# RWKV chain of a two-block layer: only the state's products stay in it, those with V and of the outputs are batched outside

## Chip, cores and metric

The program runs on one NeuronCore of one Trainium2 chip. The metric is the device time of that core in microseconds (us), as the median of several executions. All data are float32.

## What is computed

The kernel runs two transformer blocks on 512 tokens of width 1024. The first one (neighbourhood attention, gated linear attention, convolutional feed-forward) is not touched. In the second one, a projection feeds windowed attention and a bidirectional RWKV-7 time mix with 8 heads of 64; its outputs go through gates, a merge and two more feed-forward stages. The part that the change concerns is this scan, for both directions:

```python
def step(state, inp):
    r_t, w_t, k_t, v_t, a_t, b_t = inp
    sa = jnp.einsum('dbhij,dbhj->dbhi', state, a_t)
    state = (state * w_t[..., None, :] + sa[..., :, None] * b_t[..., None, :]
             + v_t[..., :, None] * k_t[..., None, :])
    y = jnp.einsum('dbhij,dbhj->dbhi', state, r_t)
    return state, y
```

The kernel does it in chunks of 64 tokens. Within a chunk the tokens' mutual effect is a triangular system, and between chunks a 64x64 state per head and direction is handed on.

## The kernel before

`block2` handles the 8 heads as four pairs `p`; the two heads `e` of a pair lie on partitions 0 to 63 and 64 to 127 (slices `H[e]`, and `O[e]` for the other half). Each pair goes through three functions.

`prep(p)` (line 1006) computes decays, keys and gates for both directions `d`. For each half of the chunks it makes `Z` (decayed queries) and `BK` (decayed keys), and their products `pP` (line 1090) on TensorE. VectorE masks these into the matrices `M[e]` (line 1092). `BKT` is `BK` transposed. The diagonal 32x32 blocks of `M` go through a DRAM scratch `scL` (line 1097) into `LF` and `XH` (lines 1112 and 1114). Then 60 VectorE operations in a row solve the triangular systems (`sx` at line 1120, `XH` at 1122). Preparation's PSUM tiles come from the pool `ps_` (tag "s", two buffers).

`finish(p)` (line 1125) writes the inverses `XH` to DRAM (`scX`) and reads them back into `M` (line 1136). It joins the 32-blocks on TensorE: `pax` (line 1144), `pt1` (1151), `pg2_` (1156). `LF` is used again here as working space.

`chain(p)` (line 1159) transposes V into `VU` (the V half; the other half takes U) and makes `W0`, the products with V (`pv`, line 1177). Then come eight dependent steps, in which direction 0 takes chunk s and direction 1 chunk 7-s:

- line 1191: `Z` times the old state `So`, into `pw`; line 1193: VectorE adds `W0`, giving `w`;
- line 1196: `M` times `w`, into `pu`; line 1199: ScalarE and VectorE copy one head each into `VU`;
- lines 1203 and 1205: an identity matmul of the old state and the product of `BKT` with `VU` (V and U at once, 128 rows) accumulate in `px`;
- lines 1226 and 1227: ScalarE and VectorE scale one direction each by the decay `PCs`, giving the new state `Sn`;
- `ymm()`: lines 1212 and 1214 make the step's outputs `py`, which lines 1218 and 1220 add into `Y`.

After the steps the outputs are normalised, transposed, gated and stored.

The order of the work is set by a list scheduler that sorts each engine's instructions by priority (program order, lowered by `low`) and readiness. It hands out the buffers of a pool's tag in program order. Program order is `prep(0)`, fill, `finish(0)`, `chain(0)`, `prep(1)`, fill, and so on. "Fill" (`fill`, line 1396) are weight matmuls at low priority: groups of `w_in_2` (line 251, 24 matmuls of 512 columns each, in two chunks of weights), and for pair 3 the `qkv` product (line 1277, 256 columns) with its norms (`qknorm`, lines 1296 to 1311). Each chunk's low part is made on GpSimd (line 203) and is loaded by SyncE's queue. After `chain(3)` comes the windowed attention (line 1313) with the last gate groups as fill.

Of the kernel before, what the change touches and what calls it, by code (L numbers as in the profile page):

```python
# [8 lines left out]
F32 = mybir.dt.float32  # L9
# [8 lines left out]
S = 512  # L18
# [138 lines left out]
class Ker:  # L157
# [768 lines left out]
    def block2(self, out):  # L926
# [79 lines left out]
        def prep(p):  # L1006
# [36 lines left out]
            for d in range(2):  # L1043
# [37 lines left out]
                for hf in ((0, 1), (1, 0))[d]:  # L1081
# [77 lines left out]
        def chain(p, st, u, PCs, XH, LF, M):  # L1159
            Y = rl.tile([128, 8, 64], F32, tag="Y", name=f"Y{p}")  # L1160
            vt = V[p]
            VU = rl.tile([128, 8, 128], F32, tag="VU", name=f"VU{p}")
            for h in range(2):
# [3 lines left out]
                for e in range(2):  # L1167
                    ev(e, VU[H[e], 4 * h:4 * h + 4, H[e]], px[:, :, H[e]])
            pbn = pc_.tile([128, 512], F32, tag="y", name=f"pbn{p}")
            nc.tensor.matmul(pbn, bones, u, start=True, stop=True)  # L1170
            nc.vector.tensor_tensor(vt, pbn, vt, ALU.mult)
            W0 = rl.tile([128, 2, 8, 64], F32, tag="W0", name=f"W0{p}")
            for d in range(2):
                pv = pc_.tile([128, 8, 64], F32, tag="y", name=f"pv{p}{d}")
                for cc in range(8):
                    for e in range(2):
                        nc.tensor.matmul(pv[O[e], cc, :], M[e][H[e], d, cc, 0:64], VU[H[e], cc, H[e]], start=True, stop=True)
                ev(d, W0[:, d], pv)
            Sn = None
            for s in range(8):  # L1180
# [26 lines left out]
                def ymm():
                    py = pc_.tile([128, 2, 64], F32, tag="y", name=f"py{p}{s}")
                    for d in range(2):
                        for e in range(2):  # L1210
                            if s > 0:
                                nc.tensor.matmul(py[H[e], d, :], zs[d][H[e], 64:128], So[H[e], d, :], start=True, stop=False)
                        for e in range(2):
# [380 lines left out]
```

## Time and profile before

| what | value |
|---|---|
| median of 3 runs | 1883.17 us |
| the runs | 1884.64, 1883.17, 1872.40 us |
| span of the profiled execution | 1873.3 us |
| busy: TensorE, VectorE, ScalarE, GpSimd | 96%, 57%, 41%, 10% of the span |

The profile is of one execution, and its span is its own time; it lies near the lowest of the three runs. Times in it are counted from the span's start. PE is the matmul part of TensorE, DVE is VectorE, ACT ScalarE, POOL GpSimd, SP SyncE, whose queue issues the DMAs. A float32 matmul shows as two records. The ends of matmuls are modelled, so their starts are read, and a busy PE need not be at its peak. PEclk is the share of full clock that TensorE was granted.

### The profile page before, as it was taken

How to read it: one execution, taken by the hardware profiler on the slowest of the kernel's cores; microseconds unless marked ns; L12 is line 12 of the kernel's file. 1: busy time of each engine (PE TensorE's matmuls, PEld its weight loads, DVE VectorE, ACT ScalarE, POOL GpSimd, SP SyncE). 2: the span in 40 equal slices, each digit the busy share in tenths (PEclk: the TensorE clock that was granted, in tenths of full speed). 3: DMA queues.
4: the chain of work that ended last, by engine and by line, in shares of the span. 5: the costliest groups of instructions: out<-in, count | busy, mean ns of one | idle time of the engine just before them, and what ended most of it. 6: DMA issues, size and time to landing. Idle time of an engine off the chain costs nothing.

```text
span 1873.3 us, 31022 instructions
## 1 busy us (share of the span) xinstructions
PE 1799.5 (96%) x11936; PEld 1506.6 (80%) x11936; DVE 1075.4 (57%) x2274; ACT 770.5 (41%) x1563; POOL 192.2 (10%) x217
## 2 busy tenths in 40 slices
PE   8999999989999999888789989999999999999998
PEld 7788888889998999866566768886678888888887
DVE  5644544787752677866746592437656553255445
ACT  6452434665442445653133432235434442234333
POOL 1000110110000001452211121112000000000000
PEclk9989989999999999998699997589999999999999
DMA  6111121653333334531221113112055333333334
GB/s 189 40 46 46 53 78 57 179 154 111 94 90 96 91 93 136 172 103 46 62 74 48 53 52 81 29 42 86 28 159 161 107 96 96 96 95 92 96 96 130
DMA packets 130789, 171.08 MB, mean 91 GB/s; under 512 B 44455, under 2 KB 59055, under 8 KB 130640
## 3 DMA queue, kind: packets, MB, share of 16 engines
q1 hardware_dynamic: 130640, 169.09, 31.1%
q8 instruction: 94, 1.54, 0.3%
q14 instruction: 55, 0.45, 0.1%
HBM read 155.42 MB, written 13.63 MB: 90 GB/s over the span
## 4 chain that ended last, share of the span: by engine, by line
PE 86%; DVE 7%; DMA 3%; issue 2%; ACT 2%; POOL 0%; SPq 0%; DVEq 0%; ACTq 0%; POOLq 0%
PE ps_w_ff L251 19%; PE ps_w_ffn_in L251 13%; PE ps_w_in L284 7%; PE ps_w_in L251 6%; PE ps_w_ffn_out L251 5%; PE ps_qkv L1277 3%; PE ps_w_out L251 2%; PE ps_w_ple_gate L251 2%; PE pP L1090 2%; PE ps_w_up_rwkv L251 1%; PE py L1214 1%; PE ps_w_up_attn L251 1%; PE ps_first L364 1%; PE paS L1350 1%; PE pS L632 1%
## 5 line engine op out<-in xcount | busy, mean ns | idle before, releaser
L203 DVE TENSOR_TENSOR wl_w_ff<-raw_w_ff,wh_w_ff 128x512 fp32r<-128x512 f32 x128 | 88.2, 689 | 131.6 <-ACT wh_w_ff L202 131.5
L202 ACT ACTIVATE wh_w_ff<-raw_w_ff 128x512 fp32r<-128x512 f32 x128 | 80.9, 632 | 194.7 <-PE ps_w_ff L251 185.9
L202 ACT ACTIVATE wh_w_in<-raw_w_in 128x512 fp32r<-128x512 f32 (+1 forms) x118 | 72.9, 623 | 101.9 <-PE ps_w_in L284 53.0
L203 POOL TENSOR_TENSOR wl_w_in<-raw_w_in,wh_w_in 128x512 fp32r<-128x512 f32 x60 | 82.0, 1371 | 254.6 <-ACT wh_w_in L202 192.2
L202 ACT ACTIVATE wh_w_ffn_in<-raw_w_ffn_in 128x512 fp32r<-128x512 f32 x96 | 60.1, 630 | 100.8 <-PE ps_w_ffn_in L251 87.4
L251 PE MATMUL ps_w_ff<-Yl,wh_w_ff 128*128 128x512 f32 x256 | 101.0, 395 | 0.0
L251 PE MATMUL ps_w_ff<-Yh,wh_w_ff 128*128 128x512 f32 x256 | 101.0, 395 | 0.0
L251 PE MATMUL ps_w_ff<-Yh,wl_w_ff 128*128 128x512 f32 x256 | 101.0, 395 | 0.0
L251 PE MATMUL ps_w_ffn_out<-Y_hi,wl_w_ffn_out 128*128 128x256 f32 (+1 forms) x256 | 83.5, 326 | 2.2 <-DVE wl_w_ffn_out L203 2.1
L251 PE MATMUL ps_w_ffn_out<-Y_hi,wh_w_ffn_out 128*128 128x256 f32 (+1 forms) x256 | 83.7, 327 | 0.0
L251 PE MATMUL ps_w_ffn_out<-Y_lo,wh_w_ffn_out 128*128 128x256 f32 (+1 forms) x256 | 83.5, 326 | 0.0
L251 PE MATMUL ps_w_ffn_in<-fa_hi,wl_w_ffn_in 128*128 128x258 f32 x352 | 73.9, 284 | 3.2 <-DVE wl_w_ffn_in L203 3.2
L203 DVE TENSOR_TENSOR wl_w_ffn_in<-raw_w_ffn_in,wh_w_ffn_in 128x512 fp32r<-128x512 f32 x96 | 65.8, 690 | 19.1 <-ACT wh_w_ffn_in L202 17.9
L251 PE MATMUL ps_w_ffn_in<-fa_hi,wh_w_ffn_in 128*128 128x258 f32 x352 | 73.8, 283 | 1.8 <-ACT wh_w_ffn_in L202 1.8
L203 DVE TENSOR_TENSOR wl_w_ffn_out<-raw_w_ffn_out,wh_w_ffn_out 128x512 fp32r<-128x512 f32 (+1 forms) x72 | 47.8, 669 | 47.7 <-ACT wh_w_ffn_out L202 47.5
L251 PE MATMUL ps_w_ffn_in<-fb_hi,wh_w_ffn_in 128*128 128x258 f32 x352 | 73.8, 284 | 0.0
L251 PE MATMUL ps_w_ffn_in<-fb_hi,wl_w_ffn_in 128*128 128x258 f32 x352 | 73.6, 283 | 0.2 <-DVE wl_w_ffn_in L203 0.2
L251 PE MATMUL ps_w_ffn_in<-fa_lo,wh_w_ffn_in 128*128 128x258 f32 x352 | 73.8, 283 | 0.0
L251 PE MATMUL ps_w_ffn_in<-fb_lo,wh_w_ffn_in 128*128 128x258 f32 x352 | 73.7, 283 | 0.0
L202 ACT ACTIVATE wh_w_ffn_out<-raw_w_ffn_out 128x512 fp32r<-128x512 f32 (+1 forms) x72 | 41.5, 582 | 62.4 <-PE ps_w_ffn_out L251 43.3
L251 PEld LDWEIGHTS ps_w_ffn_in<-fa_hi,wl_w_ffn_in 128*128 128x128 f32 x352 | 55.9, 190 | 3.6 <-DVE wl_w_ffn_in L203 3.6
L251 PEld LDWEIGHTS ps_w_ffn_in<-fa_hi,wh_w_ffn_in 128*128 128x128 f32 x352 | 55.8, 189 | 2.3 <-ACT wh_w_ffn_in L202 2.0
(645 smaller groups left out, 5274.4 us busy)
## 6 DMA issues: line engine op xcount, KB each, us to landing
raw_w_ff<-in_w_ff SPq DMA_DIRECT2D x128, 256.0 KB
raw_w_in<-in_w_in SPq DMA_DIRECT2D x116, 256.0 KB
raw_w_ffn_in<-in_w_ffn_in SPq DMA_DIRECT2D x96, 256.0 KB
raw_w_ffn_out<-in_w_ffn_out SPq DMA_DIRECT2D x40, 256.0 KB
raw_w_o<-in_w_o SPq DMA_DIRECT2D x32, 256.0 KB
raw_w_ffn_out<-in_w_ffn_out SPq DMA_DIRECT2D x32, 192.0 KB
gtd<-gt SPq DMA_DIRECT2D x16, 256.0 KB
g<-gtd SPq DMA_DIRECT2D x16, 256.0 KB
```

The source lines that it names most:

```text
L202: a = nc.scalar.activation(hi, src, AF.Copy)
L203: v = (eng or nc.vector).tensor_tensor(lo, src, hi, ALU.subtract)
L251: mm = nc.tensor.matmul(ps[si][:ncol, :s1 - s0], a[:, k, :], bk[:, s0:s1], start=(ks == k0 and k == 0 and pi == 0), stop=(ks + k == kend - ...
L284: nc.tensor.matmul(ps[:ncol, :s1 - s0], a[:, k, :], bk[:, s0:s1], start=(n == 0), stop=(n == 3 * kn - 1))
L364: nc.tensor.matmul(p[:ncol, :s1 - s0], a[:, k % 4, :], b[h][:, k % 4, s0:s1], start=(k == 0 and n == 0), stop=(k == 7 and n == 2))
L632: nc.tensor.matmul(po, pT[:, 128 * b:128 * b + 128], VW[:, 2 * ct + b, 64 * e:64 * e + 64], start=(b == 0), stop=False)
L1090: nc.tensor.matmul(pp[:, i, :], BK[rr, 4 * hf + i, :], Z[hf][rr, i, :], start=True, stop=True)
L1214: nc.tensor.matmul(py[H[e], d, :], M[e][:, d, cd[d], 64:128], VU[:, cd[d], H[e]], start=s == 0, stop=True)
L1277: nc.tensor.matmul(pq[i][:, :256], l, r[:, k - ks, :], start=(k == 0 and n == 0), stop=(k == 7 and n == 2))
L1350: nc.tensor.matmul(pS[:, :128 * nk], qT[rr, j, 128 * n:128 * n + 128], kT[rr, 128 * b0:128 * b1], start=True, stop=True)
```

## The change

The chain keeps only what depends on the state. V is transposed into its own tile `VT`, U takes the place of `W0`, the states of all chunks are kept in `PV`. Before the steps, `pk` (32 matmuls of 64x64) computes each chunk's product with V, scaled into `PV`. In a step, `px` holds only the product of `BKT` with U (64x64). VectorE makes the new state with two scalar_tensor_tensor operations on 128x64, and with two more the next step's base from it; the identity matmul is gone, and one ScalarE copy takes U. The outputs of all chunks are computed after the steps in two PSUM tiles, `pya` (tag "y") and `pyb` (pool `ps_`, tag "s"), and added into `u`'s tile. In `prep`, the `pP` matmuls of the two heads alternate.

```diff
+                    pps = [ps_.tile([128, 4, 128], F32, tag="s", name=f"pP{p}{d}{hf}{e}") for e in range(2)]
+                    for i in range(4):
+                        for e in range(2):
+                            nc.tensor.matmul(pps[e][:, i, :], BK[H[e], 4 * hf + i, :], Z[hf][H[e], i, :], start=True, stop=True)
                     for e in range(2):
-                        rr = slice(64 * e, 64 * e + 64)
-                        pp = ps_.tile([128, 4, 128], F32, tag="s", name=f"pP{p}{d}{hf}{e}")
-                        for i in range(4):
-                            nc.tensor.matmul(pp[:, i, :], BK[rr, 4 * hf + i, :], Z[hf][rr, i, :], start=True, stop=True)
...
+            PV = rl.tile([128, 2, 8, 64], F32, tag="PV", name=f"PV{p}")
             for d in range(2):
                 pv = pc_.tile([128, 8, 64], F32, tag="y", name=f"pv{p}{d}")
+                pk = ps_.tile([128, 8, 64], F32, tag="s", name=f"pk{p}{d}")
...
+                    for e in range(2):
+                        nc.tensor.matmul(pk[H[e], c, :], bkt(d, c)[H[e], H[e]], VT[H[e], c, :], start=True, stop=True)
+                nc.scalar.activation(W0[:, d], pv, AF.Copy)
+                nc.vector.tensor_tensor(PV[:, d], pk, PCs[:, d, :].rearrange("p (c o) -> p c o", o=1).to_broadcast([128, 8, 64]), ALU.mult)
+            U, SH = W0, PV
+            prev = lambda d, s: SH[:, d, (s - 1, 8 - s)[d], :]
+
+            def cross(t, s):
+                b = t[:, 0, s, :]
+                return bass.AP(b.tensor, b.offset, [list(b.ap[0]), [512 + (7 - 2 * s) * 64, 2], [1, 64]])
+
+            zc = lambda d, c: st[d][0][c // 4][:, c % 4, :]
...
-                for e in range(2):
-                    b = VU[O[e], s, H[e]]
-                    ev(e, bass.AP(b.tensor, b.offset, [list(b.ap[0]), [(7 - 2 * s) * 128, 2], [1, 64]]), pu[O[e]])
-                if s < 7:
+                nc.scalar.activation(cross(U, s), pu, AF.Copy)
+                if s == 7:
+                    continue
+                base = [PV[:, d, cd[d], :] for d in range(2)]
+                if s > 0:
+                    t = rk.tile([128, 2, 64], F32, tag="S", name=f"S{p}{s}", bufs=2)
                     for d in range(2):
+                        nc.vector.scalar_tensor_tensor(t[:, d, :], prev(d, s), PCs[:, d, cd[d]:cd[d] + 1], base[d], ALU.mult, ALU.add)
+                    base = [t[:, d, :] for d in range(2)]
+                for d in range(2):
+                    for e in range(2):
+                        nc.tensor.matmul(px[H[e], d, :], bkt(d, cd[d])[O[e], H[e]], U[O[e], d, cd[d], :], start=True, stop=True)
+                for d in range(2):
+                    nc.vector.scalar_tensor_tensor(prev(d, s + 1), px[:, d, :], PCs[:, d, cd[d]:cd[d] + 1], base[d], ALU.mult, ALU.add)
+            Y = u.rearrange("p (c v) -> p c v", c=8)
+            pya = pc_.tile([128, 8, 64], F32, tag="y", name=f"pya{p}")
+            pyb = ps_.tile([128, 8, 64], F32, tag="s", name=f"pyb{p}")
...
                         if s > 0:
-                            nc.tensor.matmul(px[:, d, :], ident, So[:, d, :], start=True, stop=False)
+                            own[e].append((zc(d, c)[H[e], 64:128], prev(d, s)[H[e]]))
+                        own[e].append((M[e][H[e], d, c, 64:128], VT[H[e], c, :]))
+                        oth[e].append((M[e][O[e], d, c, 64:128], U[O[e], d, c, :]))
+                for k in range(len(own[0])):
+                    for ps, ops in ((pya, own), (pyb, oth)):
...
+                            if k < len(ops[e]):
+                                nc.tensor.matmul(ps[H[e], c, :], *ops[e][k], start=k == 0, stop=k == len(ops[e]) - 1)
+            nc.scalar.activation(Y, pya, AF.Copy)
+            nc.vector.tensor_tensor(Y, pyb, Y, ALU.add)
```

The scheduler's order moves with it. A name's digits are the pair, then direction or step; `psw` is the first product of `prep`, `pcb` is the PSUM tile of a chain step. Each kernel has its own line numbers. First TensorE before, at the end of the products with V of pair 0:

```order
L1177 MATMUL pv01_10354<-VU0_10317,M00_9707 64x64
L1177 MATMUL pv01_10354<-VU0_10317,M01_9708 64x64
L1018 MATMUL psw10_10637<-W21_10632,TW_9629 128x256 x2
L1018 MATMUL psw11_10643<-W21_10632,TW_9629 128x256 x2
L251 MATMUL ps_w_in_2_7_10035<-ha_hi_8658,wl_w_in_2_917504_10039 128x512
L251 MATMUL ps_w_in_2_7_10035<-hb_hi_8660,wh_w_in_2_983040_10056 128x512
```

`psw10`, which opens the preparation of pair 1, follows them directly. TensorE now, in steps 0 and 1 of chain 0 (L1205 is the product with `w`, L1217 that of the state, L1200 that of the old state, L1236 the outputs):

```order
L1205 MATMUL pcb00_10408<-W00_10334,M00_9707 64x64
L1205 MATMUL pcb00_10408<-W00_10334,M01_9708 64x64
L1217 MATMUL pcb00_10408<-W00_10334,BKT000_9768 64x64 x2
L1217 MATMUL pcb00_10408<-W00_10334,BKT011_9840 64x64 x2
L1236 MATMUL pyb0_10559<-W00_10334,M00_9707 64x64
L1236 MATMUL pyb0_10559<-W00_10334,M01_9708 64x64
L1018 MATMUL psw10_10684<-W21_10679,TW_9629 128x256 x2
L1200 MATMUL pcb01_10420<-PV0_10335,Z000_9732 64x64 x2
L1200 MATMUL pcb01_10420<-PV0_10335,Z011_9805 64x64 x2
L1018 MATMUL psw11_10690<-W21_10679,TW_9629 128x256
```

`psw10` moved behind two bursts of chain 0 and the first matmuls of `pyb0`; ahead of this chain stand 146 fill matmuls in a row, between the products with V and `pax00`.

VectorE before, in steps 2 and 3 of chain 0 (`VU0`, `S02` and `w03` belong to the chain, `sx1` and `XH1` to the solve of pair 1, L1084 to the preparation of pair 2):

```order
L962 COPY VU0_10317<-pcb02_10424 64x2x64
L1122 TENSOR_TENSOR XH1_10817<-XH1_10817,sx18_10842 128x4x23
L1120 TENSOR_TENSOR sx19_10845<-XH1_10817,LF1_10816 128x110
L1122 TENSOR_TENSOR XH1_10817<-XH1_10817,sx19_10845 128x5x22
L1120 TENSOR_TENSOR sx110_10848<-XH1_10817,LF1_10816 128x105
L1227 TENSOR_SCALAR S02_10443<-pcb02_10424,PC0_9766 128x64
L1122 TENSOR_TENSOR XH1_10817<-XH1_10817,sx110_10848 128x5x21
L1120 TENSOR_TENSOR sx111_10851<-XH1_10817,LF1_10816 128x120
L1122 TENSOR_TENSOR XH1_10817<-XH1_10817,sx111_10851 128x6x20
L1193 TENSOR_TENSOR w03_10461<-pcb03_10456,W00_10335 128x128
L1120 TENSOR_TENSOR sx112_10854<-XH1_10817,LF1_10816 128x114
L1084 TENSOR_TENSOR Z200_11615<-kn2_11569,Er_9635 128x4x64
```

Operations of the chain, of the next pair's solve and of the preparation after that alternate. VectorE now, from the end of pair 0's solve into chain 0 (L1219 and L1213 are the new state operations, L1021 is preparation of pair 1):

```order
L1122 TENSOR_TENSOR XH0_9855<-XH0_9855,sx029_9943 128x15x2
L976 TENSOR_TENSOR zt0_9632<-ps_w_in_2_8_10958,rsh_75 128x512
L1120 TENSOR_TENSOR sx030_9946<-XH0_9855,LF0_9854 128x15
L988 TENSOR_TENSOR zs8_10997<-zt0_9632 128x512
L1122 TENSOR_TENSOR XH0_9855<-XH0_9855,sx030_9946 128x15
L962 COPY LF0_9854<-pax01_10228 32x512
L962 COPY LF0_9854<-pt10_10246 32x512
L962 COPY M01_9708<-pg20_10247 32x16x32
L1219 SCALAR_TENSOR_TENSOR PV0_10335<-pcb00_10408,PC0_9766,PV0_10335 128x64 x2
L1213 SCALAR_TENSOR_TENSOR S01_10432<-PV0_10335,PC0_9766 128x64 x2
L1202 TENSOR_TENSOR w01_10425<-pcb01_10420,W00_10334 128x128
L1021 TENSOR_SCALAR sw10_10683<-sw10_10683 128x512
```

The solve that stands here is that of the chain's own pair; between the chain's operations stands the preparation of the next pair, and its solve comes after it.

VectorE before, in the solve of pair 3 (with operations of chain 2):

```order
L962 COPY VU2_12241<-pcb23_12380 64x2x64
L1120 TENSOR_TENSOR sx311_12775<-XH3_12741,LF3_12740 128x120
L1122 TENSOR_TENSOR XH3_12741<-XH3_12741,sx311_12775 128x6x20
L1120 TENSOR_TENSOR sx312_12778<-XH3_12741,LF3_12740 128x114
L1122 TENSOR_TENSOR XH3_12741<-XH3_12741,sx312_12778 128x6x19
L1120 TENSOR_TENSOR sx313_12781<-XH3_12741,LF3_12740 128x126
L1227 TENSOR_SCALAR S23_12409<-pcb23_12380,PC2_11649 128x64
```

VectorE now, in the same solve (L1315 to L1320 are the norms of queries `q` and keys `k`):

```order
L1315 TENSOR_TENSOR jkq1_13388<-QT_9640,cst_61 128x64
L1122 TENSOR_TENSOR XH3_12882<-XH3_12882,sx311_12916 128x6x20
L1316 TENSOR_TENSOR jkq1_13388<-QT_9640,cst_61 128x64
L1120 TENSOR_TENSOR sx312_12919<-XH3_12882,LF3_12881 128x114
L1317 TENSOR_TENSOR jkq1_13388<-QT_9640,cst_61 128x64
L1122 TENSOR_TENSOR XH3_12882<-XH3_12882,sx312_12919 128x6x19
L1318 TENSOR_TENSOR jkq1_13388<-QT_9640,cst_61 128x64
L1120 TENSOR_TENSOR sx313_12922<-XH3_12882,LF3_12881 128x126
L1319 TENSOR_TENSOR QT_9640<-jkq1_13388 128x8x8
```

The norms moved from chain 3 into the solve, and chain 2's operations out of it.

## Rows read from the trace of the kernel before

**Rows 1.** Windows (us; busy and count by engine, PEclk, DMA share, GB/s): the chains.

```profile
970.00:1290.00 320.00, 306.31 (x2783) 232.96 (x2778) 175.79 (x497) 99.01 (x212) 56.65 (x48) 0.86 0.19 51
```

**Rows 2.** Windows, same columns: two stretches of 10 us.

```profile
900.00:910.00 10.00, 5.46 (x26) 5.08 (x27) 8.46 (x25) 0.63 (x1) 0.00 (x0) 0.50 0.05 20
1150.00:1160.00 10.00, 10.00 (x68) 8.00 (x64) 1.93 (x9) 2.05 (x7) 0.09 (x1) 0.50 0.37 116
```

**Rows 3.** Timeline (start, us, engine, line, op, out<-in [idle<-releaser]): one step of chain 3.

```profile
1252.54 0.27 PE L1191 MATMUL pcb<-S,Z 64*64 64x64 f32 x2
...
1253.04 0.29 DVE L1193 TENSOR_TENSOR w<-pcb,W 128x128 f32<-128x128 f32 x1 [1.06 <-PE pcb L1191]
...
1253.47 0.45 PE L1196 MATMUL pcb<-w,M 64*64 64x64 f32 x8
...
1253.96 0.27 ACT L962 ACTIVATE VU<-pcb 64x128 f32<-64x128 f32 x1 [1.70 <-PE pcb L1196]
...
1255.12 0.33 PE L1203 MATMUL pcb<-S,cst 128*128 128x64 f32 x2
...
1256.74 0.28 DVE L1227 TENSOR_SCALAR S<-pcb,PC 128x64 f32<-128x64 f32 x1 [2.19 <-ACT S L1226]
...
1257.27 0.28 PE L1277 MATMUL ps_qkv<-wl_w_qkv,hb_hi 128*128 128x256 f32 x1
...
1257.39 0.28 PE L1277 MATMUL ps_qkv<-wh_w_qkv,hb_lo 128*128 128x256 f32 x1
...
1257.60 0.27 PE L1191 MATMUL pcb<-S,Z 64*64 64x64 f32 x2
```

**Rows 4.** Timeline of DVE: last M, first sx, end of the solve.

```profile
873.36 0.69 DVE L1092 TENSOR_TENSOR M<-pP,cst 128x512 f32<-128x512 f32 x1
...
893.67 0.83 DVE L1120 TENSOR_TENSOR sx<-XH,LF 128x30 f32<-128x30 f32 x1 [8.65 <-DMA XH<-scL]
...
1051.28 0.69 DVE L1092 TENSOR_TENSOR M<-pP,cst 128x512 f32<-128x512 f32 x1 [0.91 <-PE pP L1090]
...
1068.99 0.18 DVE L1120 TENSOR_TENSOR sx<-XH,LF 128x30 f32<-128x30 f32 x1
...
1123.94 0.18 DVE L1122 TENSOR_TENSOR XH<-XH,sx 128x15 f32<-128x15 f32 x1
1124.41 1.29 DVE L1092 TENSOR_TENSOR M<-pP,cst 128x512 f32<-128x512 f32 x2 [0.29 <-PE pP L1090]
```

**Rows 5.** Tile sx (count: ns min/median/max, first and last start, forms).

```profile
L1120 DVE TENSOR_TENSOR sx<-XH,LF x120: 168/258/1366, 893.7 to 1206.6; 128x110 f32<-128x110 f32 x12, 128x120 f32<-128x120 f32 x12, 128x30 f32<-128x30 f32 x8, 128x56 f32<-128x56 f32 x8
```

**Rows 6.** Timeline of PE: around preparation, finish and chain.

```profile
856.74 1.12 PE L1045 MATMUL pa<-WA,A 64*128 64x512 f32 x2
...
875.05 1.15 PE L1177 MATMUL pv<-VU,M 64*64 64x64 f32 x32
...
1095.79 1.16 PE L1090 MATMUL pP<-Z,BK 64*128 64x128 f32 x8
...
1133.59 0.64 PE L1144 MATMUL pax<-cst,M 32*32 32x32 f32 x16
...
1143.92 0.47 PE L1196 MATMUL pcb<-W,M 64*64 64x64 f32 x2
...
1278.74 0.34 PE L1214 MATMUL py<-VU,M 128*64 128x64 f32 x4
```

**Rows 7.** Timeline of PE: fill matmuls at either clock level.

```profile
834.07 0.63 PE L251 MATMUL ps_w_in<-ha_hi,wl_w_in 128*128 128x512 f32 x1
834.50 0.63 PE L251 MATMUL ps_w_in<-ha_hi,wh_w_in 128*128 128x512 f32 x1
...
1093.61 0.39 PE L251 MATMUL ps_w_in<-ha_lo,wh_w_in 128*128 128x512 f32 x1
1093.83 0.40 PE L251 MATMUL ps_w_in<-ha_hi,wl_w_in 128*128 128x512 f32 x1
```

**Rows 8.** Groups of DVE by line (count | busy, mean ns | idle), 1260 to 1300.

```profile
L1302 DVE TENSOR_TENSOR QT<-QT,qkg 128x512 f32<-128x512 f32 x3 | 2.1, 684 | 0.0
```

More of the change, by code (lines that the diff above doesn't have):

```diff
@@ L1159, in chain @@
         def chain(p, st, u, PCs, XH, LF, M):
-            Y = rl.tile([128, 8, 64], F32, tag="Y", name=f"Y{p}")
             vt = V[p]
-            VU = rl.tile([128, 8, 128], F32, tag="VU", name=f"VU{p}")
+            VT = rl.tile([128, 8, 64], F32, tag="VT", name=f"VT{p}")
             for h in range(2):
@@ L1167, in chain @@
                 for e in range(2):
[L1168 removed]
+                    ev(e, VT[H[e], 4 * h:4 * h + 4, :], px[:, :, H[e]])
             pbn = pc_.tile([128, 512], F32, tag="y", name=f"pbn{p}")
@@ L1190, in chain @@
                         for e in range(2):
-                            nc.tensor.matmul(pw[O[e], d, :], zs[d][H[e], 0:64], So[H[e], d, :], start=True, stop=True)
+                            nc.tensor.matmul(pw[O[e], d, :], zc(d, cd[d])[H[e], 0:64], prev(d, s)[H[e]], start=True, stop=True)
                     w0, w = w, rk.tile([128, 2, 64], F32, tag="w", name=f"w{p}{s}", bufs=2)
@@ L1207, in ymm @@
[L1207 to L1213, printed above, removed]
-                            nc.tensor.matmul(py[H[e], d, :], M[e][:, d, cd[d], 64:128], VU[:, cd[d], H[e]], start=s == 0, stop=True)
-                    b = Y[:, s, :]
-                    yv = bass.AP(b.tensor, b.offset, [list(b.ap[0]), [(7 - 2 * s) * 64, 2], [1, 64]])
-                    if s < 4:
-                        nc.scalar.activation(yv, py, AF.Copy)
-                    else:
-                        nc.vector.tensor_tensor(yv, py, yv, ALU.add)
@@ L1222, in chain @@
-                if s == 3:
-                    ymm()
-                if s < 7:
-                    Sn = rk.tile([128, 2, 64], F32, tag="S", name=f"S{p}{s}", bufs=2)
-                    nc.scalar.activation(Sn[:, 0, :], px[:, 0, :], AF.Copy, scale=PCs[:, 0, s:s + 1])
-                    nc.vector.tensor_scalar(Sn[:, 1, :], px[:, 1, :], PCs[:, 1, 7 - s:8 - s], None, ALU.mult)
-                if s != 3:
-                    ymm()
+                nc.scalar.activation(cross(U, s), pu, AF.Copy)
@@ new lines, in chain @@
+                for d in range(2):
[3 more added lines that the diff above has]
+            pyb = ps_.tile([128, 8, 64], F32, tag="s", name=f"pyb{p}")
+            for c in range(8):
+                own, oth = [[], []], [[], []]
+                for d in range(2):
+                    s = (c, 7 - c)[d]
+                    for e in range(2):
+                        if s > 0:
+                            own[e].append((zc(d, c)[H[e], 64:128], prev(d, s)[H[e]]))
[3 more added lines that the diff above has]
+                    for ps, ops in ((pya, own), (pyb, oth)):
+                        for e in range(2):
+                            if k < len(ops[e]):
+                                nc.tensor.matmul(ps[H[e], c, :], *ops[e][k], start=k == 0, stop=k == len(ops[e]) - 1)
```

15 lines of the change are left out of this document (5 added, 10 removed).

## The prediction

> **What bounds the kernel now.** I read the stretches first. From 970 to 1290 us of the span the second block's four chains run beside weight matmuls that fill in [rows 1]. TensorE is busy for 306.3 of 320 us: it is the bound by share, though not at full speed. The granted clock is 0.86 there. Two short windows show how that comes about: half busy at 0.50 from 900 to 910, and wholly busy, still at 0.50, from 1150 to 1160 [rows 2]; 0.50 is 1.2 GHz, the lower of the two levels. So there are idle time and lost clock to win, and covered latency to lose.
>
> Next I read one step of the chain in the timeline [rows 3]. It lasts from 1252.54 to the next such matmul at 1257.60, 5.06 us. TensorE does not wait in it, because weight matmuls (line 1277) stand between the dependent ones. Without them the hops would be about 2.75 us: three bursts of four matmuls at 0.45, the sum `w` 0.29, one copy 0.27, two state operations at 0.28, and seven hand-overs at 0.05.
>
> Then I read the path that joins two pairs of heads. It runs from the last mask product `M` through DRAM to the 60 VectorE operations of the solve (`sx`, `XH`), through DRAM again to `pax`, and so to the chain. From the last `M` to the first `sx` it takes 19.6 us in pair 0 and 17.0 in pair 2 [rows 4]. The solve of pair 2 lasts from 1068.99 to 1124.12, 55 us, although one of its operations takes 0.258 us at the median [rows 5]: other work stands between them, and at a pitch of 0.29 all 60 would need 17.5. From the solve's end to `pax` it is 9.5 us, from `pax` to the chain 10.3 [rows 4, 6]. In before all this lies beside the chain of the pair ahead.
>
> **The change, part by part.** *The order is the dear part.* `pk` and `pyb` come from the two-buffer pool `ps2` (tag "s"), where preparation has its PSUM tiles too, and tiles of a tag are handed out in program order. The first excerpts show what follows: `psw10`, the first matmul of pair 1's preparation, stood right behind `pv01`, ahead of chain 0's wait for `finish(0)`. Now it stands inside chain 0, behind two bursts of it and the first use of `pyb0`. Behind that matmul waits the whole of preparation 1, and with it its DRAM trip, its solve, `finish(1)` and chain 1. The same holds for pairs 2 and 3. The second excerpts say it for VectorE: the solve of pair 1 stood among the steps of chain 0, and now a solve is over before its own chain starts. What ran side by side is done one after the other. The fill matmuls, once spread through the steps, now stand in blocks of 146, 109 and some 85 ahead of `pax`; chains 0 and 1 have none.
>
> I add up the new serial path; each term is low, taken, high, in us.
>
> - Chain, eight steps: 21, 28, 36. Low is the hop sum (the first step lacks a burst and `w`, the last the state). I take 3.5 a step, since preparation's VectorE work of 0.4 to 0.7 and two table loads on ScalarE stand between the hops.
> - Chain's end to the next pair's last `M`: 21, 27, 33. In before, pair 3's first mask product after chain 1 starts at 1095.79, and its last `M` ends at 1125.70, 29.9 later, with the same rows and some fill between [rows 4, 6]. With 3 to 4 for the outputs' batch that is the high end. Low is the 17.3 from `pa` at 856.74 to 874.05, plus 4 for what stands ahead of `pa`. I take the middle.
> - Last `M` to `sx`: 17, 18.5, 20 [rows 4].
> - Solve: 18, 23, 31. Low is alone. I add five other VectorE operations of 0.7, and some for slowed ones (the longest `sx` took 1.37 [rows 5]). High: the solve now has rows between that wait for fill groups, and 72 fills at the slow pitch of 0.43 last 31 [rows 7].
> - Solve's end to `pax` 9.5, 10, 13 and `pax` to chain 10.3, 11, 13.5: low from [rows 4, 6], high a third more, for a slow clock.
>
> A period from chain to chain is thus 97, 117.5, 147. In pair 3 the query and key norms stand between the solve's operations (third excerpts), where before they ran during chain 3. Three of their four rounds fall there, 6 us each by my estimate: three wide operations on the queries of 0.69 [rows 8], and 4 us for some eighteen small ones of the kind that `sx` is. That makes the solve 37 (32 to 46), and with 4 for that chain's fills the period is 135.5.
>
> Chain 0 can start at 874.05 + 18.5 + 23 + 10 + 11 = 936.5. Then 2 x 117.5 + 135.5 put chain 3 at 1307, and its end with the batch at 1339. In before it ends at 1279.1 [rows 6]. That is +60. Of the gate fills, 48 more are done by then; at 0.22 to 0.23 each the rest of the kernel is 11 us shorter [rows 7]. **Sum: +49 us.** All low ends together give -30, all high ends about +160.
>
> *Cheaper edits.* The identity matmuls go (14 a pair), state and output products become 64x64, `pk` adds 32. From 1255.12 to about 1256.9 a step's state and output products take 1.8 us [rows 3]. Seven such steps and the output matmuls outside that stretch are 16 us a pair. The new ones are 11: 124 in batches near 0.07, as the 16 of `pv` that take 1.15 [rows 6], and 28 in bursts near 0.1. That frees 5 us a pair. The mask products `pP` alternate between halves of the array: I value that between nothing and 17 us in all, half of four pairs' 32 at 0.27 (four take 1.16 [rows 6], a little of it the last one's end). Both shorten TensorE's work, but not a path that waits for DRAM and VectorE, so neither is in the sum. The same hides the 64x64 batch.
>
> The scalar_tensor_tensor on 128x64 does not occur in before. I bound it by the 0.28 of `TENSOR_SCALAR` on that shape and the 0.69 of a wide operation [rows 3, 8], and take 0.28. The two that form the next base lie under the next burst. At 0.69 the chain would be 6 us longer, inside its high end.
>
> The row shows that the first burst starts 0.21 after the fill ahead of it, where fills follow each other at 0.12 [rows 3]. The Trainium skill (TensorEngine Tiling (Array Packing), "Key Properties") says that switching the tiling mode drains TensorE; the trace agrees, at some 0.09 a switch. By that rule the new chain, which hardly switches, gains perhaps 20 us of TensorE work, and the sum would be +29. I leave it out, as TensorE is not what this path waits for.
>
> **The rivals.** *TensorE stays the bound.* If fills cover every wait, only its work counts: 20 to 37 us less, 28 taken, so faster, 1855. This decides it: a block of fills must last from the last `M` to `pax`, 18.5 + 23 + 10 = 51.5 us. The blocks last 34, 25 and 24 us (at 0.23, with the qkv matmuls at 0.12). Against it stand these numbers, for it only the 96% busy share of before.
>
> *The stages run at their floor.* Nothing is slowed, the solve runs alone at 18: -30 to +15, mostly no change. For it speaks that 55 us of solve become 18; against it that terms so long rarely all come out lowest.
>
> *The slow clock decides.* With TensorE waiting more, fills and bursts run at 1.2 GHz. The solve's rows then wait for fills at 0.43 (+8), chain (+6) and preparation (+3) grow, so +17 in each of three periods and +6 in chain 3: 1989. Rows 2 show both a slow clock after idling and one in a wholly busy stretch. The Trainium skill (TensorE: Matmul & The Clock Gate, "What's actually happening") says that the throttled level is the default and activity releases it; the first window agrees, the second does not fit busy time.
>
> **How the numbers follow.** The sum is made against the profiled span of 1873.3 us. The three runs are 1872.4, 1883.2 and 1884.6, so that execution was like the fastest and 9.9 below the median. Put on the median, the forecast is 1883.2 + 49 = 1932. Its own range is 1905 to 1965. About 1%, 19 us, is what a measurement of this kernel can tell from no change.
>
> Chances: forecast 0.74, slow clock 0.12, floor 0.09, TensorE bound 0.05. Slower: 0.70 of the forecast and all of the slow clock, 0.82. Same: 0.04 of the forecast and 0.06 of the floor, 0.10. Faster: 0.03 and 0.05, 0.08. For 8 in 10 the range runs from 1893 (+10) to 1978 (+95), which cuts the faster rivals and the upper half of the slow clock.
>
> **What would show it.** Right: `psw` of pairs 1 to 3 starts after the first burst of the chain ahead; TensorE's busy share between 870 and 1340 falls, with idle stretches of 10 us or more before each `pax`; chains last 25 to 36 us; a chain starts 105 to 130 us after the last; chain 3 ends near 1339. Wrong: a solve that begins within 10 us of its last `M`, TensorE busy above 90% up to chain 3, or a chain end before 1300. A single step above 4.5 us would say that VectorE's new state operations, not the lost overlap, are the price.

## The result, and the profile after

The changed kernel takes 1937.9 us in the median of four runs (1935.1 to 1944.0), the kernel before 1883.9 (1872.4 to 1884.8). The ratio is 1.0307, 95% interval 1.0273 to 1.0341. It is slower by 54 us; the forecast was 1932. The profiled execution has a span of 1933.4 us, 60.1 more than that of before.

First the stretch of the chains, in windows, with the columns of [rows 1]:

```profile
970.00:1290.00 320.00, 242.23 (x2286) 192.57 (x2285) 188.72 (x474) 93.89 (x172) 60.24 (x52) 0.80 0.19 51
```

TensorE is busy for 242.2 of 320 us, where it was 306.3: its idle time there rose from 13.7 to 77.8 us, and the granted clock went from 0.86 to 0.80. VectorE, at 188.7 us (175.8 before), is far from full. So the bound of before is gone, and no other engine has taken its place: the time is in waits. The two that matter here stand in the list of TensorE's waits between 870 and 1360 us (engine, line, waited for: total, times, longest):

```profile
PE pax L1144 <- DMA M<-scX: 26.8, 5, 16.7
...
PE pcb L1200 <- DVE PV L1219: 6.3, 8, 1.1
```

The largest of all is `pax` behind the DRAM trip of `scX`, a wait that TensorE's list of before does not have at all. The state operations of VectorE, which are new, hold TensorE for 6.3 us in all.

The order stands in TensorE's timeline at the start of chain 0 and of chain 1, and at the end of pair 3's solve:

```profile
925.89 0.47 PE L1205 MATMUL pcb<-W,M 64*64 64x64 f32 x2
...
927.85 0.69 PE L1217 MATMUL pcb<-W,BKT 64*64 64x64 f32 x8 [0.37 <-ACT W L1206]
928.33 0.42 PE L1236 MATMUL pyb<-W,M 64*64 64x64 f32 x4
928.69 1.65 PE L1018 MATMUL psw<-W,TW 65*128 65x256 f32 x3
...
963.67 0.31 PE L1205 MATMUL pcb<-w,M 64*64 64x64 f32 x1
...
1043.35 1.68 PE L1144 MATMUL pax<-cst,M 32*32 32x32 f32 x32 [5.53 <-DMA M<-scX]
...
1053.59 0.47 PE L1205 MATMUL pcb<-W,M 64*64 64x64 f32 x2
...
1296.86 1.37 PE L1144 MATMUL pax<-cst,M 32*32 32x32 f32 x24 [16.72 <-DMA M<-scX]
...
1308.67 0.31 PE L1205 MATMUL pcb<-W,M 64*64 64x64 f32 x1
```

`psw` of pair 1 starts at 928.69, behind two bursts of chain 0 and `pyb`, as the excerpt of the order had it. Chain 0 ends at 963.98, `pax` of pair 1 comes at 1043.35, and chain 1 starts at 1053.59, 127.7 us after chain 0. Before `pax` of pair 3 TensorE stands idle for 16.7 us.

What lies between is read from VectorE's timeline (pair 1: the last `M`, the solve's first and last operation):

```profile
992.22 1.29 DVE L1092 TENSOR_TENSOR M<-pP,cst 128x512 f32<-128x512 f32 x2 [0.26 <-PE pP L1089]
...
1010.99 0.71 DVE L1120 TENSOR_TENSOR sx<-XH,LF 128x30 f32<-128x30 f32 x1 [6.70 <-DMA XH<-scL]
...
1035.71 1.17 DVE L1122 TENSOR_TENSOR XH<-XH,sx 128x15 f32<-128x15 f32 x1
```

From the end of the chain to the last `M` it is 29.5 us, through DRAM 17.5, the solve 25.9, its end to `pax` 6.5. In before the last `M` of pair 1 was done at 936.9, ahead of chain 0's start at 966; now it comes at 993.5, after its end. The solve itself became short (for pair 2 it took 55.1 us in [rows 4], now 24.6), but no chain lies beside it any more, and everything waits for it.

### The profile page after: what moved, and what is told of

Its sections match the earlier page's. It is cut to its first block, busy times and chain, and to the rows that moved or that the text cites. A ratio compares the mean times of both kernels' runs of the same rounds, so it can differ in the third digit from the quotient of the medians.

```text
span 1933.4 us, 31875 instructions
## 1 busy us (share of the span) xinstructions
PE 1769.1 (92%) x12352; PEld 1492.4 (77%) x12352; DVE 1099.1 (57%) x2310; ACT 765.2 (40%) x1531; POOL 192.2 (10%) x217
## 3 DMA queue, kind: packets, MB, share of 16 engines
q1 hardware_dynamic: 130640, 169.09, 30.4%
## 4 chain that ended last, share of the span: by engine, by line
PE 76%; DVE 11%; DMA 5%; issue 4%; ACT 2%; SPq 1%; POOL 1%; DVEq 0%; ACTq 0%; POOLq 0%
PE ps_w_ff L251 18%; PE ps_w_ffn_in L251 13%; PE ps_w_in L284 7%; PE ps_w_ffn_out L251 5%; PE ps_w_in L251 2%; PE ps_w_out L251 2%; DVE sx L1120 2%; PE ps_w_ple_gate L251 2%; DMA XH<-scL 2%; DVE XH L1122 2%; PE pP L1089 1%; PE ps_w_up_rwkv L251 1%; PE ps_w_up_attn L251 1%; PE paS L1359 1%; PE ps_first L364 1%
## 5 line engine op out<-in xcount | busy, mean ns | idle before, releaser
L202 ACT ACTIVATE wh_w_ffn_in<-raw_w_ffn_in 128x512 fp32r<-128x512 f32 x96 | 60.1, 631 | 99.5 <-PE ps_w_ffn_in L251 85.6
L251 PE MATMUL ps_w_in<-ha_hi,wh_w_in 128*128 128x512 f32 (+1 forms) x136 | 55.4, 407 | 17.2 <-DVE gt L1002 9.4
L1120 DVE TENSOR_TENSOR sx<-XH,LF 128x30 f32<-128x30 f32 (+7 forms) x120 | 42.3, 352 | 42.8 <-DMA XH<-scL 39.7
```

Of the source, the lines that this page charges most:

```text
L202: a = nc.scalar.activation(hi, src, AF.Copy)
L251: mm = nc.tensor.matmul(ps[si][:ncol, :s1 - s0], a[:, k, :], bk[:, s0:s1], start=(ks == k0 and k == 0 and pi == 0), stop=(ks + k == kend - ...
L1120: nc.vector.tensor_tensor(sv, XH[:, 0:k, t:t + 1].to_broadcast([128, k, n]), LF[:, t:t + 1, t + 1:32].to_broadcast([128, k, n]), ALU.mult)
```

## The experiments

*The order alone, undone.* One word is changed in the changed kernel:

```diff
-            pyb = ps_.tile([128, 8, 64], F32, tag="s", name=f"pyb{p}")
+            pyb = pc_.tile([128, 8, 64], F32, tag="c", name=f"pyb{p}")
```

> The changed kernel with one word moved: pyb takes its PSUM tile from the chain's own pool (tag "c") and not from preparation's (tag "s"). Lost overlap: psw of pair 1 stands ahead of the chain again, the solve of a pair runs beside the chain ahead of it, and the time falls under the kernel before, since TensorE has 0 to 37 us less to do: 1850 to 1885 us, 1865 taken; chains start some 90 us apart. Rival, the new work in the chain (VectorE's state operations, the products in a batch) is the price: the order of preparation is nothing, 1920 to 1940 us. Rival, the slow clock by itself: as the new work, with a granted clock under 0.8 between 880 and 1170 us.

Measured: 1864.8 us, ratio to before 0.9943 (0.9907 to 0.9979). The whole loss of 54 us is gone by one PSUM tag, while every operation of the new chain is still there. The new work is therefore not the price; that rival falls. The slow clock by itself, which was to give the same 1920 to 1940 us with under 0.8 granted between 880 and 1170 us, falls too: 0.84 was granted there. Chains start at 955.7, 1029.6, 1168.3 and 1236.6: periods of 74, 139 and 68 us, 94 on the mean, where some 90 each had been expected.

That long one has its own cause, seen in TensorE's timeline of this kernel ahead of chain 1:

```profile
1020.60 1.06 PE L1165 MATMUL pvs<-cst,zv 128*64 128x128 f32 x4
1021.59 2.03 PE L1181 MATMUL pk<-VT,BKT 64*64 64x64 f32 x32
...
1025.80 1.02 PE L1181 MATMUL pk<-VT,BKT 64*64 64x64 f32 x26
...
1027.73 1.13 PE L1018 MATMUL psw<-W,TW 65*128 65x256 f32 x4
```

`pk` of pair 1 also takes its tile from preparation's pool and stands ahead of `psw` of pair 2 there. It needs `VT`, which the transposes `pvs` fill, and `VT` has one buffer, which chain 0 reads to its end. So `psw` of pair 2 starts only at 1027.73, right behind `pk`.

*`pk` moved as well.*

```diff
-                pk = ps_.tile([128, 8, 64], F32, tag="s", name=f"pk{p}{d}")
+                pk = pc_.tile([128, 8, 64], F32, tag="c", name=f"pk{p}{d}")
```

> As pyb_c, and pk too takes tag "c". Lost overlap: pk ran ahead of the chain in any case, so it holds little back; 1850 to 1885 us, within 10 us of pyb_c. New work in the chain: 1920 to 1940 us.

Measured: 1829.1 us (1827.7 to 1831.8), ratio 0.9736 (0.9683 to 0.9789). That is 36 us below `pyb_c`, where within 10 had been expected: a miss, since I had looked at pair 0 alone, in which `pk` does run early. The stretch of the chains in this kernel, and `psw` of pair 2 in its timeline, which now stands even ahead of `pax` of pair 0 (945.19):

```profile
970.00:1290.00 320.00, 290.47 (x3326) 221.32 (x3327) 212.30 (x604) 111.77 (x245) 59.58 (x51) 0.92 0.22 59
```

```profile
933.54 1.89 PE L1018 MATMUL psw<-W,TW 65*128 65x256 f32 x8
...
945.19 0.64 PE L1144 MATMUL pax<-cst,M 32*32 32x32 f32 x16
```

TensorE is busy for 290.5 of 320 us at a granted clock of 0.92. This kernel beats before by 48 us and the changed one by 109.

*`pk` alone.* The second edit without the first.

> The changed kernel with only pk moved to tag "c", pyb left in tag "s". Lost overlap by pyb: no change against the changed kernel, 1925 to 1950 us. If pk is what holds preparation back: under 1910 us.

Measured: 1935.0 us, ratio 1.0299 (1.0237 to 1.0361). As expected: while `pyb` holds preparation back, `pk` costs nothing. One wait hides the other.

*The order alone, put into the kernel before.*

```diff
-                    py = pc_.tile([128, 2, 64], F32, tag="y", name=f"py{p}{s}")
+                    py = ps_.tile([128, 2, 64], F32, tag="s", name=f"py{p}{s}") if s == 0 else pc_.tile([128, 2, 64], F32, tag="y", name=f"py{p}{s}")
```

> The kernel before with one word added: the output tile py of step 0 alone comes from preparation's pool (tag "s"), so that psw of the next pair must stand inside the chain; nothing else of the change. Lost overlap: the whole loss is there without any of the new work, and somewhat more, since the chain's steps still hold the identity matmuls and the outputs: 1935 to 1970 us, periods of 125 to 140 us. New work in the chain, or the slow clock by itself: the kernel before, 1870 to 1900 us.

Measured: 2002.7 us, ratio 1.0643 (1.0557 to 1.0729). The loss is there without any of the new work, so it is shown from both sides. It is larger than expected, 33 us over the upper end. The window of chain 0 in this kernel, and one step of it (starts of two `Z` bursts):

```profile
930.30:989.50 59.20, 56.25 (x384) 41.19 (x382) 18.14 (x46) 12.72 (x29) 0.00 (x0) 0.50 0.02 4
```

```profile
979.01 0.37 PE L1191 MATMUL pcb<-S,Z 64*64 64x64 f32 x2
...
980.36 0.69 PE L1196 MATMUL pcb<-w,M 64*64 64x64 f32 x8
...
987.40 0.37 PE L1191 MATMUL pcb<-S,Z 64*64 64x64 f32 x2
```

The old chain, with preparation in it and no fill, takes 59.2 us and not the 38 of the new one. TensorE is busy for 56.3 of these at 0.50 of its clock, and the step shown lasts 8.4 us: products of preparation (`pP` and `pbk`, some 3.7 us of it) and between them the chain's identity matmuls, outputs and products of 128 rows, all at 1.2 GHz. Here the new chain's smaller work does lie on the path; its share beside the alternating `pP` was not measured by itself.

*Preparation kept out of the chain.* The changed kernel with `pya`, too, in preparation's pool, so that both its buffers are held until the outputs are done.

```diff
-            pya = pc_.tile([128, 8, 64], F32, tag="y", name=f"pya{p}")
+            pya = ps_.tile([128, 8, 64], F32, tag="s", name=f"pya{p}")
```

> The changed kernel with pya too in preparation's pool (tag "s"), so that both its buffers are held until the outputs are done and preparation can't stand inside the chain at all. If the preparation between the hops is what stretched chains 0 and 1 to 38 us: 27 to 31 us a chain; if the low clock is: 35 us or more still. Either way preparation comes after the chain as a whole, some 48 us from psw to the last M in place of the 29 us left behind the chain now: 1960 to 2010 us.

Measured: 1954.1 us, 6 under the lower end expected; ratio 1.0387 (1.0312 to 1.0462). Chains 0 and 1 take 26.6 us each (926.5 to 953.1 and 1060.1 to 1086.7), just under the 27 to 31 of the first reading, where the changed kernel takes 38.1 and 38.5. The windows of chain 0 here, and of the changed kernel's chain 0:

```profile
926.50:953.10 26.60, 16.29 (x201) 12.36 (x200) 8.37 (x34) 1.94 (x7) 0.00 (x0) 0.50 0.00 1
```

```profile
926.00:964.00 38.00, 32.34 (x263) 23.94 (x265) 17.51 (x53) 8.56 (x17) 0.00 (x0) 0.54 0.01 3
```

The granted clock is 0.50 in the one and 0.54 in the other, so the clock is not what makes the difference. One step in the timeline, first here, then in the changed kernel:

```profile
937.09 0.69 PE L1200 MATMUL pcb<-PV,Z 64*64 64x64 f32 x8 [0.74 <-DVE PV L1219]
937.82 0.29 DVE L1202 TENSOR_TENSOR w<-pcb,W 128x128 f32<-128x128 f32 x1 [0.49 <-PE pcb L1200]
...
938.17 0.69 PE L1205 MATMUL pcb<-w,M 64*64 64x64 f32 x8 [0.38 <-DVE w L1202]
938.91 0.28 ACT L1206 ACTIVATE W<-pcb 128x128 f32<-128x128 f32 x1 [3.29 <-PE pcb L1205]
...
939.24 0.69 PE L1217 MATMUL pcb<-W,BKT 64*64 64x64 f32 x8 [0.38 <-ACT W L1206]
940.04 0.48 DVE L1219 SCALAR_TENSOR_TENSOR PV<-pcb,PC,S 128x64 f32<-128x64 f32 x2 [1.93 <-PE pcb L1217]
...
940.67 0.69 PE L1200 MATMUL pcb<-PV,Z 64*64 64x64 f32 x8 [0.74 <-DVE PV L1219]
```

```profile
935.80 0.69 PE L1200 MATMUL pcb<-PV,Z 64*64 64x64 f32 x8 [0.74 <-DVE PV L1219]
936.43 1.86 PE L1030 MATMUL pkn<-cst,ksq 128*128 128x2 f32 x8
938.22 0.69 PE L1205 MATMUL pcb<-w,M 64*64 64x64 f32 x8
939.45 0.80 PE L1038 MATMUL pkr<-cst,knb 128*128 128x128 f32 x2 [0.53 <-ACT knb L1035]
940.18 0.69 PE L1217 MATMUL pcb<-W,BKT 64*64 64x64 f32 x8
940.80 1.65 PE L1038 MATMUL pkr<-cst,knb 128*128 128x128 f32 x6
942.38 0.69 PE L1200 MATMUL pcb<-PV,Z 64*64 64x64 f32 x8
```

Bare, a step takes 3.58 us. With preparation it takes 6.58: in front of each dependent burst stands a product of preparation of 0.8 to 1.9 us (`pkn`, `pkr`). It isn't wasted, for from the chain's end to the last `M` it is then 29.5 us and not the 48.3 of this kernel (953.1 to 1001.5).

*TensorE made busier.* The changed kernel with two matmuls on constants more behind each burst of a step (into unused columns; nobody reads them). These two lines stand behind each of the three bursts:

```diff
+                for _ in range(2):
+                    nc.tensor.matmul(pcb[:, 384:512], ident, ident, start=True, stop=True)
```

> The changed kernel with two matmuls of 128x128 more behind each of a step's bursts (six a step, on constants, into unused columns of pcb, read by no one), to see what a chain takes if TensorE is busier. Chains 0 and 1 took 38 us at a granted clock of 0.50 to 0.54. If the low clock is what stretches them and the added work raises it: granted clock over 0.8 in the chains, 30 to 35 us a chain, 1920 to 1937 us in all. If the preparation between the hops stretches them, or the clock doesn't rise: the added 6 x 0.2 to 0.45 a step come on top, 45 us a chain or more, 1955 to 1990 us.

Measured: 1973.6 us, ratio 1.0504 (1.0429 to 1.0579). The granted clock in chain 0 rose only to 0.74 (window from 926 to 970), and that chain grew from 38 to 46.6 us. The times are those of the second reading: more work on this path costs time even where TensorE has waits. But the clock stayed under the 0.8 that the first reading asked for, so it is `a_serial`, and not this run, that tells the two apart.

*Parts of the change by themselves.* Four kernels price the edits that the forecast left out of its sum. `pkpyb_noPP` is `pkpyb_c` with the mask products in the old order:

```diff
-                    for i in range(4):
-                        for e in range(2):
-                            nc.tensor.matmul(pps[e][:, i, :], BK[H[e], 4 * hf + i, :], Z[hf][H[e], i, :], start=True, stop=True)
...
+                        for i in range(4):
+                            nc.tensor.matmul(pp[:, i, :], BK[rr, 4 * hf + i, :], Z[hf][rr, i, :], start=True, stop=True)
```

> As pkpyb_c (1829 us), but the mask products pP of the two heads no longer alternate. If alternation saves TensorE's time alone, as the prediction valued it: 0 to 17 us more, 1829 to 1846. If the last M, and with it each solve, also comes some 7 us earlier a pair by it (866.8 against 874.1 in pair 0): 1850 to 1865 us.

Measured: 1852.8 us (1843.7 to 1866.3), 24 above `pkpyb_c`; ratio 0.9859 (0.9761 to 0.9957), an interval that overlaps a little with that of `pkpyb_c`. Alternation shortens the path too: from the first `psw` that the trace shows to the last `M` of pair 0 it takes 44.6 us in `pkpyb_c` (824.8 to 869.3), 50.0 here (826.8 to 876.8). These two are near the extremes: over all kernels of this case it is 44.6 to 47.1 us with alternation and 47.6 to 50.0 without, some 3 us apart on the mean. `b_pP` is the reverse, the kernel before with the first hunk of the change alone:

> The kernel before with one part of the change alone: the mask products pP of the two heads alternate. Beside pkpyb_c they were worth 24 us. If that holds by itself: 1850 to 1860 us. If it needs the short chain beside it (since before, TensorE is the bound and the solve is spread by other work): 1865 to 1880.

Measured: 1860.2 us, ratio 0.9948 (0.9907 to 0.9990). By the ratio that is a gain of some 10 us, 2 to 17 by its interval, on the border of what the two readings expected: how large it is is not settled.

`b_stt` is the kernel before with the identity matmul replaced alone:

```diff
-                        if s > 0:
-                            nc.tensor.matmul(px[:, d, :], ident, So[:, d, :], start=True, stop=False)
...
+                    if s > 0:
+                        t = rk.tile([128, 2, 64], F32, tag="w", name=f"T{p}{s}", bufs=2)
+                        for d in range(2):
+                            nc.vector.tensor_scalar(t[:, d, :], So[:, d, :], PCs[:, d, cd[d]:cd[d] + 1], None, ALU.mult)
...
+                            nc.vector.scalar_tensor_tensor(Sn[:, d, :], px[:, d, :], PCs[:, d, cd[d]:cd[d] + 1], t[:, d, :], ALU.mult, ALU.add)
```

> The kernel before with one part of the change alone: no identity matmul; VectorE scales the old state and adds it (tensor_scalar and scalar_tensor_tensor, in steps 1 to 7), V and U still in one product of 128 rows, outputs in the steps. If TensorE's work is what counts in the overlapped order: 14 identity matmuls a pair go, 56 x 0.13 to 0.38 us, 7 to 21 us less, 1856 to 1870. If VectorE's operations lengthen the steps by more than they free: 1877 or more.

Measured: 1875.8 us, ratio 0.9984 (0.9953 to 1.0014): no change, and a time between the two ranges. In the chains' stretch (970 to 1290 us) TensorE's busy time falls from 306.3 to 299.5 us, and the time does not follow. `pkpyb_ident` puts the identity matmul back into `pkpyb_c`:

```diff
...
-                    for d in range(2):
-                        nc.vector.scalar_tensor_tensor(t[:, d, :], prev(d, s), PCs[:, d, cd[d]:cd[d] + 1], base[d], ALU.mult, ALU.add)
...
+                    if s > 0:
+                        nc.tensor.matmul(px[:, d, :], ident, prev(d, s), start=True, stop=False)
```

> As pkpyb_c (1829 us), with the identity matmul back in steps 1 to 7 (it adds the old state in px; VectorE's two operations for the step's base go, the two that scale px and add V's part stay). In the kernel before, taking the identity matmul out alone changed nothing measurable (1876 beside 1878). If it counts here no more than there: 1824 to 1835 us. If it counts by its time on TensorE and by its two changes of tiling a step, now that the steps are otherwise all 64x64: 14 a pair at 0.13 to 0.38 us and 14 changes at 0.09, 12 to 26 us more, 1841 to 1855 us.

Measured: 1844.3 us (1841.3 to 1853.8), 15 above `pkpyb_c`; ratio 0.9839 (0.9783 to 0.9895). So much the same edit is worth nothing in the old chain and some 15 us in the new one, though the intervals of the ratios of `pkpyb_c` and `pkpyb_ident` still overlap by a hair (0.9789 and 0.9783).

*Two other splits of the fill.* Both start from `pkpyb_c`: `best_a` takes two more groups of gate matmuls beside the pairs, `best_c` one fewer, `(3, 2, 4, 1)`:

```diff
-        W = (3, 2, 4, 2)
+        W = (3, 3, 4, 3)
```

> As pkpyb_c (1829 us), with one more group of gate matmuls to fill in beside pairs 1 and 3 each (W = 3, 3, 4, 3 in place of 3, 2, 4, 2), since TensorE still waits some 45 us between 870 and 1290. If the fills go into that: up to 10 us less, 1819 to 1826. If they stand in front of dependent matmuls: 1829 to 1845.

> As pkpyb_c (1829 us), with one group of gate matmuls fewer beside pair 3 (W = 3, 2, 4, 1). If the groups beside pair 3 stand in front of its dependent matmuls: 1820 to 1827 us. If they lie in waits: 24 matmuls at 0.22 come later, 1832 to 1838 us.

Measured: 1843.1 us with more (ratio 0.9877, 0.9795 to 0.9959), 1829.9 with fewer (0.9745, 0.9701 to 0.9789). Neither beats `pkpyb_c`; the second lies between its two ranges. The 14 us with more fills are in the range of the second reading, but that the fills stand in front of dependent matmuls is not shown: in the profiled executions 8 of the 18 us between the two kernels stand ahead of the first `psw` (832.9 against 824.8), where their work is the same.

## Why the forecast held, and where its terms did not

The mechanism was the one forecast: the tile `pyb` in preparation's pool moves the next pair's preparation behind the start of the chain, and what lay side by side comes one after the other. Undoing that one tag gives the loss back (1864.8), and it alone makes the loss in the kernel before (2002.7).

The terms, as forecast and as the trace after has them (us; pairs 0 to 1, 1 to 2, 2 to 3):

| term | forecast | measured |
|---|---|---|
| chain 0 starts at | 936.5 | 925.9 |
| chain | 28 (+4 fills in chain 2) | 38.1, 38.5, 33.4 |
| chain's end to last `M` | 27 | 29.5, 28.4, 30.4 |
| last `M` to `sx` | 18.5 | 17.5, 17.0, 20.0 |
| solve | 23, 23, 37 | 25.9, 24.6, 28.4 |
| solve's end to `pax` | 10 | 6.5, 6.0, 6.9 |
| `pax` to chain | 11 | 10.2, 9.5, 11.8 |
| period | 117.5, 117.5, 135.5 | 127.7, 124.0, 131.0 |
| chain 3 starts, outputs done | 1307, 1339 | 1308.7, 1340.6 |

The end came out to 1.6 us, but by errors that cancel. Over the three periods the chain was 22 us longer than its term, the way from it to the last `M` 7 longer; `pax` came 11 sooner after the solve, the other terms together 6, and chain 0 started 11 earlier. Half of these 11 is luck of the execution: the first `psw` came at 821.0 us where before had it at 826.5, though the same 5804 matmuls stand ahead of it (over the kernels of this case it comes between 817 and 833).

- *Chain.* This is the term that was mis-sized: 28 a chain, with 36 as the high end, and two measured above that. Both of its parts were short. The hops of one step add up to 2.82 us by the prediction's own terms (it writes 2.75), and the whole chain to the low end of 21; bare, in `a_serial`, a step takes 3.58 and the chain 26.6. The bursts make that difference: in the step of [rows 3] four matmuls take 0.45, at a granted clock of 1.00 by the window below (of before), and in the bare chain 0.69 at 0.50. And what I had added for the preparation between the hops, some 0.7 a step, was 11.5 / 8 = 1.4. I had counted its VectorE operations and table loads; the trace shows its matmuls on TensorE, at half clock, in front of the bursts.

```profile
1252.50:1257.60 5.10, 5.10 (x59) 4.05 (x58) 0.86 (x3) 1.50 (x4) 1.26 (x1) 1.00 0.00 2
```

- *A step above 4.5 us* was named as the sign that VectorE's state operations are the price. Steps of 6.6 us occurred, and the sign was badly chosen: the operations themselves take what was forecast, as VectorE's groups by form show:

```profile
L1219 DVE SCALAR_TENSOR_TENSOR PV<-pcb,PC,S 128x64 f32<-128x64 f32 x48 | 11.4, 278 | 31.2 <-PE pcb L1217 31.2
L1213 DVE SCALAR_TENSOR_TENSOR S<-PV,PC 128x64 f32<-128x64 f32 x48 | 11.3, 276 | 0.0
```

- *Solve.* In pair 3 I took 37 and it is 28.4; the norms between its operations cost less than the 6 us a round of the estimate, which had added up their times. From one operation of the solve on 128x110 to the next it is 0.31 us where nothing stands between (VectorE's timeline in pair 1) and 0.32 where a norm operation of 0.21 does (in pair 3):

```profile
1030.32 0.27 DVE L1122 TENSOR_TENSOR XH<-XH,sx 128x110 f32<-128x110 f32 x1
1030.63 0.28 DVE L1120 TENSOR_TENSOR sx<-XH,LF 128x110 f32<-128x110 f32 x1
...
1282.41 0.26 DVE L1122 TENSOR_TENSOR XH<-XH,sx 128x110 f32<-128x110 f32 x1
1282.59 0.21 DVE L1316 TENSOR_TENSOR jkq<-QT,cst 128x64 f32<-128x64 f32 x1
1282.73 0.26 DVE L1120 TENSOR_TENSOR sx<-XH,LF 128x110 f32<-128x110 f32 x1
```

  In pairs 0 to 2 the solve is 25 to 27 and not 23. Its slow operations stand beside GpSimd's work: all 25 that took over 0.6 us, of the 240 in the four solves, overlap a tensor operation of GpSimd (timeline of both engines):

```profile
886.44 2.55 POOL L203 TENSOR_TENSOR wl_w_in<-raw_w_in,wh_w_in 128x512 fp32r<-128x512 f32 x2 [1.91 <-ACT wh_w_in L202]
886.51 1.30 DVE L1122 TENSOR_TENSOR XH<-XH,sx 128x54 f32<-128x54 f32 x1
...
887.84 1.25 DVE L1120 TENSOR_TENSOR sx<-XH,LF 128x78 f32<-128x78 f32 x1
...
889.12 0.24 DVE L1122 TENSOR_TENSOR XH<-XH,sx 128x78 f32<-128x78 f32 x1
```

- *Rest of the kernel.* I took 11 us off for 48 fills done earlier. There are 48 fewer, but from the outputs of chain 3 to the end it is 592.8 us where it was 594.2. Up to the first `paS` of the attention it is 20.0 us in before and 21.9 now, though 31 fills stand there and not 66 (windows of before and of the changed kernel, with the columns of [rows 1]):

```profile
1279.10:1299.10 20.00, 18.75 (x87) 14.20 (x87) 12.83 (x40) 10.76 (x19) 6.74 (x6) 1.00 0.44 125
1340.60:1362.50 21.90, 13.66 (x51) 9.56 (x49) 8.45 (x14) 9.94 (x15) 2.73 (x2) 0.77 0.29 97
```

  TensorE now waits there for 8.2 us (1.3 before): for the norm of the outputs, for a gate and for the queries (`pyt` 2.4, `u` 1.4, `pgt` 0.9, `pqT` 3.5), which the missing fills used to cover, and its granted clock is 0.77 where it was 1.00. That cancels the gain. It is most of the error that is left: +60 in the profiled executions against the +49 of the sum (+54 by the medians).
- *The marks.* `psw` behind the first burst, the lower busy share and the end near 1339 came as said. An idle stretch of 10 us or more came only ahead of pair 3's `pax` (16.7; in pairs 0 to 2 it was 2.5, 5.5 and 1.6), because the blocks of fill, with the waits in them, lasted 43, 38 and 39 us (871.3 to 914.0 in pair 0), where I had counted 34, 25 and 24. Two marks were missed by a little: chains were to last 25 to 36 us (38.1 and 38.5 are above), and to start 105 to 130 us apart (the last period is 131.0).
- *The rivals.* "TensorE stays the bound" named the right condition, a cover of the whole solve, and the fills did not give it. Where the overlap is kept, its result comes about, and better than its 20 to 37 us: `pkpyb_c` gains 48. I had undersized it: by the exchanges above, the alternation and the identity matmul bring some 24 and 15 us there; the batched outputs, V's products and the still earlier preparation were not tried by themselves. "The slow clock decides" named a part of the price and not its cause. The clock did drop (0.54 and 0.50 in chains 0 and 1), and its +6 a chain is what the bare chain shows over the hops (26.6 against 21); of its +3 for preparation 1 to 3 came. Its +8 for the solve did not: that grew by 2 to 3 us in pairs 1 and 2, beside GpSimd's work, and stayed under its term in pair 3. Undoing the order takes the whole loss away, so the order is the cause. What the low clock adds to preparation's matmuls between the bursts no run separates.
- *The two tags.* The prediction named `pk` and `pyb` together. `pyb` alone sets the loss; `pk` costs 36 us, but only once `pyb` is out of the way.

The change is thus two things of opposite sign. By the medians, with an order like that of after, everything else in it, alternation included, is worth 65 us (2002.7 to 1937.9). With overlap, 48 (1877.1 to 1829.1). The order costs 126 us with the old chain and, both tags together, 109 with the new one.

## What to carry to other kernels

When a change adds a tile to a pool, look at who else takes buffers from that tag, and where in program order: a tile that is used late holds back everything that is allotted after it, whatever engine that runs on. Then count what the held-back work used to lie beside, stage by stage, and add the stages up as a serial path; a lower busy share of the busiest engine is no gain if the stages that it covered are now waited for. And move such tiles one by one: the second held-back tile shows only when the first is gone.

## What the runs showed of the hardware that was not expected

The mask products of the two heads take half the time when they alternate. In [rows 6] eight records, the four products of one head, take 1.16 us (line 1090). The timeline of `pkpyb_c` has sixteen records, the products of both heads, in the same time and at the same granted clock (1.00 in both windows); each head uses its own half of the rows (operands on 64 partitions):

```profile
845.75 1.16 PE L1089 MATMUL pP<-Z,BK 64*128 64x128 f32 x16 [1.95 <-DVE Z L1085]
```

The Trainium skill (TensorEngine Tiling (Array Packing), "Key Properties") says that tiles operate independently and can run matmuls in parallel; the trace agrees, 16 records in 1.16 us against 8.

The granted clock stayed at 0.50 through the 59.2 us of chain 0 of `b_py0`, although TensorE is recorded as busy for 56.3 of them; before that stretch it had waited for `pax`. The Trainium skill (TensorE: Matmul & The Clock Gate, "What's actually happening") says that activity releases the throttle; this stretch, like that of [rows 2] from 1150 to 1160, does not fit busy time as the records count it, and no run here settles what it goes by. A forecast of this serial path would have done better to take its TensorE work at 1.2 GHz.
